# All stores from the memory stage to the end of cross-attention, issued by GpSimd instead of SyncE

## The chip, the cores and the metric

The kernel is one layer of an encoder block, written for one core of a Trainium2 chip. The core has a matrix engine (PE), a vector engine (DVE), a scalar engine (ACT), GpSimd (POOL) and SyncE (SP), which run on their own and meet at semaphores, and 16 DMA engines that move data between HBM and the on-chip memory. The metric is device time in microseconds of one launch, on one core. Each engine works through a list of instructions that is fixed when the program is built, strictly in its order: an instruction that has to wait holds up all that stand behind it on the same engine.

## The reference

The sequence has 2048 positions of width 1024, the memory 256 positions, and there is one layer. All of it is float32.

```
h  = rms_norm(x, mix_norm);  z = h @ w_in
cb, cc, cu, q, k, v, g, lr_f, lr_b = split_cols(z)
y_conv = grouped_rms_norm(cb * dwconv3(cc * cu))
o      = bidirectional_gla(q/8, k, v, log_sigmoid(lr_f @ w_af + b_af)/16, log_sigmoid(lr_b @ w_ab + b_ab)/16)
x += concat[y_conv, rms_norm(o) * silu(g)] @ w_out
kv = rms_norm(mem, mem_norm) @ w_xkv
x += softmax(rms_norm(x, xa_norm) @ w_xq . k_mem / 16) . v_mem @ w_xo        # 4 heads
x += square(relu(rms_norm(x, mlp_norm) @ w_up)) @ w_down
out = rms_norm(x, final_norm)
```

## The kernel before

Every float32 product is made of three products of a faster 32-bit format: each operand is split into a high and a low part (`split`, L115 to L118: ACT makes the high part, DVE the low one), and `mm3` (L143 to L147) issues high·high, high·low and low·high. So a weight goes from HBM into a raw tile (`load_w`, L129 to L134, the DMA is L131), through ACT and DVE, and then to PE.

The stages follow one another on PE:

- the memory stage, keys: `kv_mm` and `xa_key` for four heads make a matrix zA in HBM (8 tiles of 128x256 a head, each scaled by ACT in L565 and stored in L566). Beside it the first half of x is loaded (`load_T`, L176), squared (L184) and normalised (`block_rows`, `block_steps`).
- the first half of the projections: `qk` stores zk and zq (L234), `vg` and `lr_g` store zg and zv (`vg_store`, L253), `conv` stores zy (L371).
- the memory stage, values: `kv_mm` and `xa_value` make zO (L579 copies, L581 stores), beside it the second half of x.
- the second half of the projections, then gated linear attention for four heads (`gla_states`, `gla_out`): it reads zk, zq, zv and zg back (L420, L440, L499), runs a scan over chunks on DVE (L474), and stores zy (L515). The second half of `conv` is laid between its steps.
- the output projection with the residual, which stores x1d (L920, L908), cross-attention, which stores x2d (L731, L746), then the feed-forward layer and the last norm.

What sets the order: inside `tc.manual_schedule` the engines that it names follow the order in which the code is written; elsewhere, and for the engines it does not name, a scheduler that runs when the program is built puts the instructions of each engine in order, by costs of its own. SP issues every DMA of the kernel before the change, loads and stores, in one list. POOL has little to do in the first 2000 us: the step of the inverse root mean square in `rstd_of` (L151, L153), which takes 4 columns at a time.

Buffers come in rings by tag. A tile is given out again when all that read it are done, a store included when it has landed. The raw ring (`RAW`) has 3 buffers, `T2`, from which most stored tiles come, has 7, `GT` has 8.

Of the kernel before, what the change touches and what calls it, by code (L numbers as in the profile page):

```python
# [17 lines left out]
P = 128  # L18
# [3 lines left out]
TB = 512  # L22
EPS = 1e-6
NMEM = 256
# [6 lines left out]
def block_kernel(ctx, tc, x, mem, wm, wv, wlg, wlog, wout, wxk, wxv, wxqT, wxo, wup, wdn,  # L31
                 vecs, ones, consts, out):
    nc = tc.nc
# [70 lines left out]
    zy = [dram.tile([P, S], F32, name=f"zy{i}") for i in range(8)]  # L104
    zA = dram.tile([D, 1024], F32, name="zA")
    zO = dram.tile([1024, D], F32, name="zO")
# [120 lines left out]
    def qk(hf, blks, ws):  # L227
        t0 = hf * 1024
        for pr in range(2):
            for z, idx, sc in ((zk, 2 + pr, 1.0), (zq, pr, 0.125)):  # L230
                def ev(bi, ps, z=z, sc=sc):
                    t = T2()
                    nc.scalar.mul(t, ps, sc)
                    nc.sync.dma_start(z[pr][:, t0 + bi * TB:t0 + (bi + 1) * TB], t)  # L234
                mtiles([(idx, ev)], blks, ws)
                ws = None

# [8 lines left out]
    def vg_store(hf, t, ps, z, c, func):  # L246
        st = T2()[:, :256]
        if func is AF.Copy:
            nc.vector.tensor_copy(st, ps)  # L249
        else:  # L250
            nc.scalar.activation(st, ps, func)
        tok = hf * 1024 + t * P
        nc.sync.dma_start(z[tok:tok + P, c * 256:(c + 1) * 256], st)  # L253

    VG = ((zg, 1), (zv, 0), (zv, 1))

# [49 lines left out]
    def conv(hf, blks, cs, ws=None, meanwhile=None):  # L306

        n0 = 1022 if hf == 0 else 1026
        off = 1 if hf == 0 else 3
        a0 = 0 if hf == 0 else 1022  # L310

        def group(c, ws):
            HP, T = CV(), CV()
            if hf == 0:
                nc.vector.memset(HP[:, 0:1], 0.0)
            else:
                nc.vector.tensor_copy(HP[:, 0:3], save[:, c, 0:3])
                nc.vector.memset(HP[:, 1027:1028], 0.0)

            def ev_c(bi, ps):  # L320
                nc.scalar.copy(HP[:, off + bi * TB:off + (bi + 1) * TB], ps)

            def ev_u(bi, ps):
                sl = HP[:, off + bi * TB:off + (bi + 1) * TB]
                nc.vector.tensor_tensor(out=sl, in0=ps, in1=sl, op=ALU.mult)
                if bi == 1:
                    taps()

            def taps():

                nc.vector.tensor_scalar_mul(T[:, :n0], HP[:, 0:n0], cw[:, 3 * c:3 * c + 1])
                for tap in (1, 2):
                    nc.vector.scalar_tensor_tensor(out=T[:, :n0], in0=HP[:, tap:tap + n0],
                                                   scalar=cw[:, 3 * c + tap:3 * c + tap + 1],
                                                   in1=T[:, :n0], op0=ALU.mult, op1=ALU.add)
                if hf == 0:
                    nc.vector.tensor_copy(save[:, c, 0:3], HP[:, 1022:1025])
                else:
                    nc.vector.tensor_tensor(out=T[:, 0:2], in0=T[:, 0:2], in1=save[:, c, 4:6], op=ALU.mult)

            held = []

            def ev_b(bi, ps):
                if hf == 0 and c == 3 and bi == 0:
                    held.append(ps)
                    return
                for bj, pb in enumerate(held + [ps], start=bi - len(held)):
                    if hf == 0:
                        n = TB if bj == 0 else TB - 2
                        sl = T[:, bj * TB:bj * TB + n]  # L350
                        if bj == 1:
                            nc.vector.tensor_copy(save[:, c, 4:6], pb[:, TB - 2:TB])
                    else:
                        n = TB
                        sl = T[:, 2 + bj * TB:2 + (bj + 1) * TB]
                    nc.vector.tensor_tensor(out=sl, in0=pb[:, :n], in1=sl, op=ALU.mult)

            tiles = [(4 + 3 * c, ev_c), (5 + 3 * c, ev_u), (6 + 3 * c, ev_b)]
            if hf == 0 and c == 3:
                mtiles(tiles, blks)  # L360
            else:
                for t in tiles:
                    mtiles([t], blks, ws)
                    ws = None
                    if meanwhile and c == cs[-1]:
                        next(meanwhile, None)
            return T

        for c in cs:
            T = group(c, ws if c == cs[0] else None)  # L370
            nc.sync.dma_start(zy[c][:, a0:a0 + n0], T[:, :n0])  # L371


    def gla_decay(h, res):
# [103 lines left out]
    def gla_out(h, Q, K, St):  # L478
        ats, ys = [None] * 4, [None] * 4

        def attn(j):
            pf, pb = PG((P, 4, P)), PG((P, 4, P))
            for c in range(4):
                hf, sl = chunk(4 * j + c)
                nc.tensor.matmul(pf[:, c], K[hf][0:64, sl], Q[hf][0:64, sl], start=True, stop=True)
                nc.tensor.matmul(pb[:, c], K[hf][64:128, sl], Q[hf][64:128, sl], start=True, stop=True)
            at = ats[j] = GT(F32, (P, 4, P))
            nc.scalar.copy(at, pb)
            nc.vector.copy_predicated(at, maskf, pf)

        def outp(j):
            v = load_v(h, j)
            po = PG((P, 4, P))
            for c in range(4):
                hf, sl = chunk(4 * j + c)
                nc.tensor.matmul(po[:, c], Q[hf][:, sl], St[:, 4 * j + c], start=True, stop=False)
                nc.tensor.matmul(po[:, c], ats[j][:, c], v[:, c], start=False, stop=True)
            sg = GT(F32, (P, 4, P))
            nc.sync.dma_start(sg, zg[j * TB:(j + 1) * TB, h * P:(h + 1) * P].rearrange("(c p) d -> p c d", p=P))  # L499
            y = ys[j] = GT(F32, (P, 4, P))  # L500
            nc.scalar.activation(y, po, AF.Square)
            ss = GS(4)
            nc.vector.tensor_reduce(out=ss, in_=y, op=ALU.add, axis=AX.X)
            r = rstd_of(ss, 4, P, GS)
            for c in range(4):
                nc.vector.scalar_tensor_tensor(out=y[:, c], in0=po[:, c], scalar=r[:, c:c + 1], in1=sg[:, c],
                                               op0=ALU.mult, op1=ALU.mult)

        def fin(j):
            pt = PG((P, 4, P))  # L510
            for c in range(4):
                nc.tensor.transpose(pt[:, c], ys[j][:, c], ident)
            yt = GT(F32, (P, 4, P))
            nc.scalar.mul(yt, pt, g_gla)
            nc.sync.dma_start(zy[4 + h][:, j * TB:(j + 1) * TB], yt.rearrange("p c t -> p (c t)"))  # L515
        return attn, outp, fin


# [37 lines left out]
    def xa_key(h, K, T):  # L556
        kh, kl = K
        w = [load_w(wxqT[2 * h + j], T=T) for j in range(2)]
        for dt in range(KT):
            sl = slice(dt * P, (dt + 1) * P)  # L560
            ps = PS()
            for j in range(2):
                mm3(ps[:, :NMEM], (w[j][0][:, sl], w[j][1][:, sl]), (kh[:, j], kl[:, j]), j == 0, j == 1)
            st = T2()
            nc.scalar.activation(st[:, :NMEM], ps[:, :NMEM], AF.Copy, scale=g_xa[:, dt:dt + 1])  # L565
            nc.sync.dma_start(zA[sl, h * NMEM:(h + 1) * NMEM], st[:, :NMEM])  # L566

    def xa_value(h, V, T):
        vh, vl = V
        w = [load_w(wxo[2 * h + j], T=T) for j in range(2)]  # L570
        for m in range(2):
            for n in range(2):
# [5 lines left out]
                st = T2()  # L578
                nc.scalar.copy(st, ps)  # L579
                row = h * NMEM + m * P  # L580
                nc.sync.dma_start(zO[row:row + P, ns], st)  # L581

    def y_tiles(b, kp):
        if b == 2 and kp < 2:
# [58 lines left out]
    SB = 256  # L643
# [77 lines left out]
    def xa_out(s, q):  # L721
        L = live[s]
        xt = L["xs"][q]
        for i in range(4):
# [3 lines left out]
                ph, pl = L["p"][kt // 2]  # L728
                mm3(ps, (wO[kt][0][:, ds], wO[kt][1][:, ds]), (ph[:, kt % 2], pl[:, kt % 2]), kt == 0, kt == KT - 1)
            nc.vector.tensor_tensor(out=xt[:, i], in0=ps, in1=xt[:, i], op=ALU.add)  # L730
        nc.sync.dma_start(x2d[q * TB:(q + 1) * TB, s * SB:(s + 1) * SB].rearrange("(k p) t -> p k t", p=P), xt)  # L731

    def xa_last(s):
        L = live[s]
# [7 lines left out]
        for q in range(2):  # L742
            xt = L["xs"][q]
            for i in range(4):
                nc.vector.tensor_tensor(out=xt[:, i], in0=pss[4 * q + i], in1=xt[:, i], op=ALU.add)
            nc.sync.dma_start(x2d[q * TB:(q + 1) * TB, s * SB:(s + 1) * SB].rearrange("(k p) t -> p k t", p=P), xt)  # L746

    XR = lambda i: RAW((P, 2, TB)) if i % 2 == 0 else CV()[:, :D].rearrange("p (j t) -> p j t", j=2)

# [141 lines left out]
    for b in range(4):  # L891
        bs = slice(b * TB, (b + 1) * TB)
        yb, nxt = nxt, []
        if b == 3:
# [10 lines left out]
                    mm3(pss[d], (wo[kt][0][:, ds], wo[kt][1][:, ds]), yb[kt // 2][kt % 2], kt == 0, kt == KT - 1)  # L905
            for d in range(KT):
                nc.vector.tensor_tensor(out=xts[d], in0=pss[d], in1=xts[d], op=ALU.add)
                nc.sync.dma_start(x1d[d * P:(d + 1) * P, bs], xts[d])  # L908
            continue
        for dp in range(KT // 2):  # L910
            ld = y_load(b + 1, dp)
            xt = load_T(x, b, dp, CV()[:, :D].rearrange("p (j t) -> p j t", j=2))
            for j in range(2):
# [3 lines left out]
                for kt in range(KT):  # L917
                    mm3(ps, (wo[kt][0][:, ds], wo[kt][1][:, ds]), yb[kt // 2][kt % 2], kt == 0, kt == KT - 1)
                nc.vector.tensor_tensor(out=xt[:, j], in0=ps, in1=xt[:, j], op=ALU.add)
                nc.sync.dma_start(x1d[ds, bs], xt[:, j])  # L920
            nxt.append(y_split(b + 1, dp, *ld))

    row = lambda z, kt: z[kt * P:(kt + 1) * P, :]
# [488 lines left out]
```

## Time and profile before

| what | value |
|---|---|
| time, median of 3 runs (lowest to highest) | 2677.62 us (2676.23 to 2678.01) |
| time of the profiled execution | 2673.82 us |
| its span | 2672.0 us |
| PE busy | 2580.3 us, 97% of the span |
| DVE, ACT, POOL busy | 61%, 35%, 10% |
| granted clock of PE, mean over the span | 0.988 |
| DMA queue of SP | 351.05 MB, 40.2% of 16 engines' span |
| POOL instructions | 178 in all |

The profile comes from one execution of the program; the span is the time between its first and last instruction, and some 2 us lie around it. "Busy" counts instructions of the engine itself, and not what its sequencer does: waits and the issue of DMAs show in rows marked with a q (SPq). In the timeline a row gives the start in us from the beginning of the span, the duration, engine and line, operation, the tiles written and read, and in square brackets the idle time just before it with what ended it; "x5" means that five instructions were merged into the row, with the duration from the first start to the last end.

### The profile page before, as it was taken

The numbers are of one execution on the slowest core, as the hardware profiler recorded it, in microseconds if no ns is written. First come the engines' busy times: TensorE is split into PE (matmuls) and PEld (weight loads), VectorE is DVE, ScalarE is ACT, GpSimd is POOL, SyncE is SP. The second block draws the span as 40 slices with busy tenths as digits, with TensorE's granted clock in tenths as the row PEclk, the third lists the DMA queues.
The fourth block names the chain that finished last, engine by engine and source line by source line (L and its number), as shares of the span: only waits on it lengthen the run. The fifth ranks groups of instructions, "written<-read, shape, count | busy, mean of one in ns | idle before, by whom it ended". The sixth has DMA issues, their size and how long they took to land.

```text
span 2672.0 us, 34688 instructions
## 1 busy us (share of the span) xinstructions
PE 2580.3 (97%) x13560; PEld 2199.2 (82%) x13560; DVE 1627.1 (61%) x2502; ACT 934.0 (35%) x1432; POOL 259.9 (10%) x178
## 2 busy tenths in 40 slices
PE   7999999989989999999999999999999999999998
PEld 7898888877777787999997888788887888888887
DVE  6512364367766555444468566865555768788887
ACT  6411143334435443232225333443333323222322
POOL 0000000000000000000000000000002324243233
PEclk9999999999999999999999999999999999999999
DMA  7512355234445453110125333343328664555232
GB/s 258 179 60 67 107 175 174 74 91 127 123 117 171 146 181 111 46 50 33 64 79 185 115 107 114 111 161 111 122 99 309 229 196 156 179 162 183 95 116 106
DMA packets 198308, 353.26 MB, mean 132 GB/s; under 512 B 17344, under 2 KB 73792, under 8 KB 198144
## 3 DMA queue, kind: packets, MB, share of 16 engines
q1 hardware_dynamic: 198144, 351.05, 40.2%
q8 instruction: 106, 1.74, 0.3%
q14 instruction: 58, 0.48, 0.1%
HBM read 262.90 MB, written 88.08 MB: 131 GB/s over the span
## 4 chain that ended last, share of the span: by engine, by line
PE 79%; DVE 10%; DMA 5%; ACT 3%; issue 2%; POOL 1%; SPq 0%; DVEq 0%; POOLq 0%; ACTq 0%
PE ps L1016 12%; PE pg L1260 10%; PE ps L1260 10%; PE ps L145 9%; PE ps L147 9%; PE ps L146 9%; PE pg L1016 9%; PE pg L145 2%; PE pg L146 2%; PE pg L147 2%; DVE a L118 2%; DMA gt<-zv 1%; DVE st L474 1%; DMA raw<-zy 1%; DVE a L928 1%
## 5 line engine op out<-in xcount | busy, mean ns | idle before, releaser
L145 PE MATMUL ps<-a,a 128*128 128x512 f32 (+1 forms) x840 | 306.1, 364 | 6.4 <-DVE t L249 5.9
L146 PE MATMUL ps<-a,a 128*128 128x512 f32 (+1 forms) x840 | 306.0, 364 | 0.0
L147 PE MATMUL ps<-a,a 128*128 128x512 f32 (+1 forms) x840 | 305.0, 363 | 0.0
L1260 PE MATMUL pg<-a,g 128*128 128x512 f32 x1176 | 285.8, 389 | 3.6 <-DVE a L928 1.2
L1016 PE MATMUL ps<-a,g 128*128 128x512 f32 x1152 | 282.6, 390 | 2.5 <-DVE a L118 1.4
L1260 PE MATMUL ps<-a,g 128*128 128x512 f32 x1176 | 284.9, 389 | 0.0
L1016 PE MATMUL pg<-a,g 128*128 128x512 f32 x1152 | 278.4, 389 | 1.7 <-ACT g L117 1.1
L1260 PEld LDWEIGHTS pg<-a,g 128*128 128x128 f32 x1176 | 220.4, 188 | 51.3 <-ACT a L117 2.8
L1260 PEld LDWEIGHTS ps<-a,g 128*128 128x128 f32 x1176 | 220.7, 188 | 45.8
L1016 PEld LDWEIGHTS ps<-a,g 128*128 128x128 f32 x1152 | 215.9, 188 | 48.5 <-DVE a L118 2.1
L1016 PEld LDWEIGHTS pg<-a,g 128*128 128x128 f32 x1152 | 215.9, 188 | 48.1 <-ACT g L117 2.0
L117 ACT CAST a<-raw 128x1024 fp32r<-128x1024 f32 (+1 forms) x128 | 130.0, 1022 | 331.2 <-PE ps L1260 102.6
L118 DVE TENSOR_TENSOR a<-raw,a 128x1024 fp32r<-128x1024 f32 (+1 forms) x128 | 156.3, 1228 | 122.9 <-ACT a L117 121.1
L117 ACT CAST g<-gt 128x512 fp32r<-128x512 f32 x180 | 103.8, 618 | 334.8 <-PE pg L1016 192.8
L145 PEld LDWEIGHTS ps<-a,a 128*128 128x128 f32 x840 | 161.5, 192 | 32.6 <-DVE t L249 4.7
L147 PEld LDWEIGHTS ps<-a,a 128*128 128x128 f32 x840 | 161.8, 193 | 23.2
L146 PEld LDWEIGHTS ps<-a,a 128*128 128x128 f32 x840 | 161.8, 193 | 23.2 <-issue 0.2
L118 DVE TENSOR_TENSOR g<-gt,g 128x512 fp32r<-128x512 f32 x180 | 129.7, 758 | 49.1 <-ACT g L117 49.0
L928 DVE TENSOR_TENSOR t<-pg,t 128x512 f32<-128x512 f32 x64 | 44.2, 690 | 166.6 <-issue 127.9
L153 POOL TENSOR_TENSOR sm<-sm,nhalf 128x2 f32<-128x2 f32 (+1 forms) x26 | 24.3, 933 | 991.2 <-DVE sm L151 991.2
L118 DVE TENSOR_TENSOR g<-raw,g 128x1024 fp32r<-128x1024 f32 (+3 forms) x90 | 98.6, 1106 | 34.8 <-ACT g L117 34.6
L117 ACT CAST g<-raw 128x1024 fp32r<-128x1024 f32 (+3 forms) x90 | 85.4, 959 | 97.6 <-PE ps L146 17.7
(325 smaller groups left out, 5203.0 us busy)
## 6 DMA issues: line engine op xcount, KB each, us to landing
raw<-zu SPq DMA_DIRECT2D x64, 512.0 KB, 4.0
t<-in_wdn SPq DMA_DIRECT2D x84, 256.0 KB, 3.7
raw<-in_wm SPq DMA_DIRECT2D x32, 512.0 KB, 4.0
raw<-in_wup SPq DMA_DIRECT2D x32, 512.0 KB, 4.1
cv<-in_wup SPq DMA_DIRECT2D x32, 512.0 KB, 5.0
zu<-gt SPq DMA_DIRECT2D x64, 256.0 KB, 2.3
zu<-t SPq DMA_DIRECT2D x64, 256.0 KB, 3.9
cv<-zu SPq DMA_DIRECT2D x32, 512.0 KB, 5.1
```

The source lines that it names most:

```text
L117: mark["act"] = nc.scalar.copy(hi, src)
L118: nc.vector.tensor_tensor(out=lo, in0=src, in1=hi.bitcast(F32), op=ALU.subtract)
L145: nc.tensor.matmul(ps, lh, rh, start=first, stop=False)
L146: nc.tensor.matmul(ps, lh, rl, start=False, stop=False)
L147: mark["pe"] = nc.tensor.matmul(ps, ll, rh, start=False, stop=last)
L153: nc.gpsimd.tensor_tensor(out=r, in0=v, in1=nhalf[:, :n], op=ALU.pow)
L474: nc.vector.scalar_tensor_tensor(out=St[r, a], in0=St[r, b], scalar=de[r, a:a + 1], in1=St[r, a], op0=ALU.mult, op1=ALU.add)
L928: eng.tensor_tensor(out=out, in0=a, in1=b, op=op)
L1016: nc.tensor.matmul(ps, W[w][:, ks], X[x][kt], start=first and kt + w + x == 0, stop=kt == 3 and w == 1, skip_group_check=not first)
L1260: nc.tensor.matmul(ps, l, r, start=not chained and k == 0 and l is wh and r is x[k][0], stop=k == n - 1 and l is wl, skip_group_check=chained)
```

## The change

Ten `dma_start` calls move from `nc.sync` to `nc.gpsimd`: those that store zk and zq, zg and zv, zy (two places), zA, zO, x1d (two places) and x2d (two places). These are 200 DMAs at run time. The stores of the feed-forward layer (zu) and of the output stay on SP. Nothing else is edited.

```diff
-                    nc.sync.dma_start(z[pr][:, t0 + bi * TB:t0 + (bi + 1) * TB], t)
+                    nc.gpsimd.dma_start(z[pr][:, t0 + bi * TB:t0 + (bi + 1) * TB], t)
...
-        nc.sync.dma_start(z[tok:tok + P, c * 256:(c + 1) * 256], st)
+        nc.gpsimd.dma_start(z[tok:tok + P, c * 256:(c + 1) * 256], st)
...
-            nc.sync.dma_start(zy[c][:, a0:a0 + n0], T[:, :n0])
+            nc.gpsimd.dma_start(zy[c][:, a0:a0 + n0], T[:, :n0])
...
-            nc.sync.dma_start(zy[4 + h][:, j * TB:(j + 1) * TB], yt.rearrange("p c t -> p (c t)"))
+            nc.gpsimd.dma_start(zy[4 + h][:, j * TB:(j + 1) * TB], yt.rearrange("p c t -> p (c t)"))
...
-            nc.sync.dma_start(zA[sl, h * NMEM:(h + 1) * NMEM], st[:, :NMEM])
+            nc.gpsimd.dma_start(zA[sl, h * NMEM:(h + 1) * NMEM], st[:, :NMEM])
...
-                nc.sync.dma_start(zO[row:row + P, ns], st)
+                nc.gpsimd.dma_start(zO[row:row + P, ns], st)
...
-        nc.sync.dma_start(x2d[q * TB:(q + 1) * TB, s * SB:(s + 1) * SB].rearrange("(k p) t -> p k t", p=P), xt)
+        nc.gpsimd.dma_start(x2d[q * TB:(q + 1) * TB, s * SB:(s + 1) * SB].rearrange("(k p) t -> p k t", p=P), xt)
...
-                nc.sync.dma_start(x1d[d * P:(d + 1) * P, bs], xts[d])
+                nc.gpsimd.dma_start(x1d[d * P:(d + 1) * P, bs], xts[d])
...
-                nc.sync.dma_start(x1d[ds, bs], xt[:, j])
+                nc.gpsimd.dma_start(x1d[ds, bs], xt[:, j])
```

How the lists of the engines change shows in three places. The first is SP's list in the memory stage for values, where the second quarter of x is loaded (a_3223 to a_3232, from in_x), the four tiles of one head are stored into zO, and the weights of the next head come in (in_wxv, in_wxo). Lines with a minus stand in the list before, lines with a plus in the list after.

```order
 L176 DMA a_3232<-in_x 128x512 x2
-L581 DMA zO<-t_3190 128x512
-L131 DMA raw<-in_wxv 128x1024
-L581 DMA zO<-t_3200 128x512
-L581 DMA zO<-t_3210 128x512
-L131 DMA raw<-in_wxv 128x1024
-L581 DMA zO<-t_3220 128x512
-L131 DMA raw<-in_wxo 128x1024 x3
+L131 DMA raw<-in_wxv 128x1024 x2
+L131 DMA raw<-in_wxo 128x1024 x4
```

The loads keep their order among themselves, and no store stands between them any more. In the memory stage for keys SP's list changes in the same way (zA, in_wxk, in_wxqT, in_x).

The second place is POOL's list in the memory stage for keys, around the inverse root mean square (L153) that belongs to the second quarter of x. The stores ahead of it are those of the third head, the ones behind it those of the fourth; before, the four rows of L153 with 4 columns stood there with nothing between them.

```order
+L566 DMA zA<-t_740 128x256
+L566 DMA zA<-t_750 128x256
+L566 DMA zA<-t_760 128x256
+L153 TENSOR_TENSOR sm<-sm,nhalf 128x4
+L566 DMA zA<-t_828 128x256
+L566 DMA zA<-t_838 128x256
```

Now L153 comes after the last of eight stores of one head. In the stage for values it stands behind the twelfth store of zO in the same way.

The third place is DVE's list in the attention, at the scan of the last head (L474; L489 copies a masked product, L603 to L635 belong to the norm of the first block of zy). Before:

```order
L474 SCALAR_TENSOR_TENSOR st<-st,gs 64x128 x8
L489 COPY_PREDICATED gt<-cst,pg 128x512
L474 SCALAR_TENSOR_TENSOR st<-st,gs 64x128
L603 TENSOR_TENSOR t_6857<-t_6857,ps 128x512
L474 SCALAR_TENSOR_TENSOR st<-st,gs 64x128
L489 COPY_PREDICATED gt<-cst,pg 128x512
L474 SCALAR_TENSOR_TENSOR st<-st,gs 64x128
L604 TENSOR_SCALAR t_6857<-t_6857 128x512
L474 SCALAR_TENSOR_TENSOR st<-st,gs 64x128
L605 TENSOR_TENSOR t_6833<-t_6857,t_6833 128x512
```

And after, at the same place:

```order
L474 SCALAR_TENSOR_TENSOR st<-st,gs 64x128 x8
L489 COPY_PREDICATED gt<-cst,pg 128x512
L474 SCALAR_TENSOR_TENSOR st<-st,gs 64x128 x3
L489 COPY_PREDICATED gt<-cst,pg 128x512
L474 SCALAR_TENSOR_TENSOR st<-st,gs 64x128 x6
L503 TENSOR_REDUCE gs<-gt 128x4
```

The norm's instructions no longer stand between the steps of the scan; they come after it. PE's list changes too, in the attention alone: pieces of the convolution's matmuls stand a little earlier or later between the attention's. From cross-attention on, the lists of PE and DVE are as they were.

More of the change, by code (lines that the diff above doesn't have):

```diff
@@ L745, in xa_last @@
                 nc.vector.tensor_tensor(out=xt[:, i], in0=pss[4 * q + i], in1=xt[:, i], op=ALU.add)
-            nc.sync.dma_start(x2d[q * TB:(q + 1) * TB, s * SB:(s + 1) * SB].rearrange("(k p) t -> p k t", p=P), xt)
+            nc.gpsimd.dma_start(x2d[q * TB:(q + 1) * TB, s * SB:(s + 1) * SB].rearrange("(k p) t -> p k t", p=P), xt)
     XR = lambda i: RAW((P, 2, TB)) if i % 2 == 0 else CV()[:, :D].rearrange("p (j t) -> p j t", j=2)
```

## The prediction

> **What bounds the kernel now.** I read the busy time of each engine by stage first. The columns are the stage in us, its length, then busy us and instructions of PE, PE's weight loads, DVE, ACT and POOL, then the granted clock of PE, the share of the DMA engines and GB/s.
>
> ```profile
> 0.00:75.00 75.00, 55.33 (x387) 52.76 (x388) 50.75 (x68) 47.39 (x70) 2.91 (x7) 0.93 0.75 244
> 75.00:350.00 275.00, 274.97 (x1585) 244.56 (x1585) 78.57 (x112) 54.09 (x76) 0.00 (x0) 0.99 0.30 97
> 350.00:400.00 50.00, 45.23 (x291) 41.79 (x290) 35.63 (x41) 31.69 (x41) 2.02 (x2) 0.93 0.69 231
> 500.00:850.00 350.00, 313.51 (x1914) 265.15 (x1914) 240.87 (x480) 142.44 (x190) 21.53 (x32) 0.97 0.41 123
> ...
> 1050.00:1350.00 300.00, 299.91 (x1977) 271.68 (x1976) 136.27 (x309) 89.86 (x204) 10.67 (x12) 1.00 0.14 46
> 1350.00:2672.00 1322.00, 1298.22 (x6026) 1080.03 (x6024) 943.05 (x1276) 447.51 (x672) 221.38 (x123) 1.00 0.45 148
> ```
>
> PE is the bound wherever it has data: in the 275 us after 75 and in cross-attention (1050 to 1350) it is idle for 0.1 us at most, so 60 of the 200 moved stores (44 of the first half's projections and the 16 of x2d) lie where nothing can be gained. The idle time that the change can reach is in the two memory stages (0 to 75, where the first 11 us are the first loads; 350 to 400) and in the attention (36.5 us in 500 to 850). The last row, half of the kernel, is not touched.
>
> An idle gap costs more than itself. I asked for the clock right behind four of the gaps named below:
>
> ```profile
> 44.60:47.90 3.30, 3.27 (x15) 3.27 (x16) 0.00 (x0) 1.80 (x4) 0.00 (x0) 0.51 0.40 137
> 61.70:65.00 3.30, 3.30 (x18) 3.30 (x17) 3.30 (x5) 1.66 (x5) 0.00 (x0) 0.50 0.87 278
> 382.50:389.20 6.70, 6.05 (x26) 5.76 (x27) 5.83 (x7) 4.17 (x6) 0.00 (x0) 0.51 0.73 251
> 795.60:798.90 3.30, 3.11 (x14) 3.14 (x15) 3.20 (x6) 0.93 (x2) 0.00 (x0) 0.50 0.00 0
> ```
>
> PE runs at half its clock there, for 3.3 or 6.7 us, so such a gap loses another 1.65 or 3.35 us.
>
> **Term 1, weights of the key stage: -4.2 us.** The rows are splits of weights on DVE, then SP's list, then rows of PE that open with an idle gap.
>
> ```profile
> 30.47 2.35 DVE L118 TENSOR_TENSOR a<-raw,a 128x1024 fp32r<-128x1024 f32 x2
> 33.26 1.23 DVE L118 TENSOR_TENSOR a<-raw,a 128x1024 fp32r<-128x1024 f32 x1 [0.44 <-ACT a L117]
> ...
> 36.94 1.23 DVE L118 TENSOR_TENSOR a<-raw,a 128x1024 fp32r<-128x1024 f32 x1 [1.86 <-ACT a L117]
> ```
>
> ```profile
> 31.72 0.33 SPq L131 DMA_DIRECT2D raw<-in_wxk  x1
> 32.14 2.87 SPq L566 DMA_DIRECT2D zA<-t  x5
> 35.10 0.89 SPq L131 DMA_DIRECT2D raw<-in_wxqT  x2
> ...
> 48.41 1.18 SPq L566 DMA_DIRECT2D zA<-t  x2
> 49.68 0.45 SPq L131 DMA_DIRECT2D raw<-in_wxqT  x1
> ```
>
> ```profile
> 42.08 0.39 PE L145 MATMUL ps<-t,g 128*128 128x256 f32 x1 [1.91 <-ACT g L117]
> 43.34 0.39 PE L147 MATMUL ps<-t,g 128*128 128x256 f32 x1 [0.76 <-DVE g L118]
> 44.63 0.58 PE L147 MATMUL ps<-t,g 128*128 128x256 f32 x1 [0.67 <-DVE g L118]
> ...
> 59.52 0.39 PE L145 MATMUL ps<-t,g 128*128 128x256 f32 x1 [0.72 <-ACT g L117]
> 60.78 0.39 PE L147 MATMUL ps<-t,g 128*128 128x256 f32 x1 [0.76 <-DVE g L118]
> ```
>
> A weight load needs a raw buffer, which the DVE half of an earlier split frees. For the two loads at 35.10 and 35.58 the buffers came free at 32.8 and 34.5, while SP stood at five stores of zA. Without these the second, on which PE's gap before 44.6 ends, goes 1.1 us earlier. The load at 49.68 stood behind a store that waited for ACT; its buffer had been free for some 11 us (the split that ends at 38.17). So both gaps at 58.7 to 60.8 (0.72 + 0.76 = 1.48) go, with the half clock behind them (1.65). Bounds: nothing, and 8.1 if all of the gaps from 40 on went (1.91 + 0.76 + 0.67 = 3.34, and 1.48, and two windows of 1.65).
>
> **Term 2, weights of the value stage: -6.3 us.**
>
> ```profile
> 367.92 4.26 SPq L176 DMA_DIRECT2D a<-in_x  x8
> 375.93 0.33 SPq L581 DMA_DIRECT2D zO<-t  x1
> 376.35 0.38 SPq L131 DMA_DIRECT2D raw<-in_wxv  x1
> ...
> 375.34 0.56 ACT L579 COPY t<-ps 128x512 f32<-128x512 f32 x1
> ```
>
> ```profile
> 382.69 0.58 PE L145 MATMUL ps<-gt,g 128*128 128x256 f32 x1 [2.96 <-ACT g L117]
> ```
>
> SP was free at 372.2 and then waited 3.8 us to store a tile that ACT copied only at 375.34. The load behind it carries the weights for which PE then idles 2.96 us. Issued at 372.2 it lands 4.1 us earlier, which covers the gap and, with it, the 6.7 us of half clock. Bounds: nothing (if the raw buffer is late), and 6.3.
>
> **Term 3, loads of the attention: -2.8 us.**
>
> ```profile
> 548.48 14.12 SPq L253 DMA_DIRECT2D zv<-t  x6
> 566.33 15.31 SPq L440 DMA_DIRECT2D gt<-zv  x5
> 571.94 1.13 PE L465 MATMUL pg<-gt 128*128 128x128 f32 x8 [1.55 <-DMA gt<-zv]
> 758.82 1.14 SPq L515 DMA_DIRECT2D zy<-gt  x1
> 765.79 0.49 PE L497 MATMUL pg<-gt 128*128 128x128 f32 x2 [2.56 <-DMA gt<-zv]
> ```
>
> The first load of zv stood behind stores of zv that follow PE's pace for 14 us; it can go well before 566, and the gap of 1.55 goes. Of the gap of 2.56 the store at 758.82 accounts for 1.2 (1.14 and the issue around it). The other gaps there end on DVE, on POOL's root mean square, or on loads that waited for their own buffer, so they stay. Bounds: nothing, and 4.1 (both gaps).
>
> **Term 4, the scan of the last head: -6.0 us.**
>
> ```profile
> 782.61 3.02 DVE L474 SCALAR_TENSOR_TENSOR st<-st,gs 64x128 f32<-64x128 f32 x8
> 795.29 0.35 DVE L474 SCALAR_TENSOR_TENSOR st<-st,gs 64x128 f32<-64x128 f32 x1
> 795.79 0.76 PE L496 MATMUL pg<-st,g 128*128 128x128 f32 x2 [4.38 <-DVE st L474]
> ```
>
> The scan took from 782.61 to 795.64, as the list before has a step of the norm after each step of the scan. In the list after, 17 steps at 3.02/8 = 0.38 us and two L489 of 0.76 end 8.0 us after the start, at 790.6, ahead of PE's gap (791.4). So the 4.38 us go, and the half clock behind them (1.65). Bounds: nothing (if what is now behind the scan is late instead), and 6.0.
>
> **Cost 1, POOL's stores: +4.2 us.** No row shows a DMA that POOL issues. The first row below is from the list of PE's waits, the last from the DMA issues (KB each, us from issue to landing). Call x the time by which such a store is later done than SP's.
>
> ```profile
> PE pg L169 <- POOL sm L153: 5.7, 4, 1.8
> ```
>
> ```profile
> 69.17 1.01 POOL L153 TENSOR_TENSOR sm<-sm,nhalf 128x4 f32<-128x4 f32 x1 [27.71 <-DVE sm L151]
> ...
> 61.99 6.94 SPq L566 DMA_DIRECT2D zA<-t  x8
> ...
> zA<-t SPq DMA_DIRECT2D x32, 128.0 KB, 3.0
> ```
>
> First, the stored tiles of zA come from a ring of seven, two of which hold the head's keys; five are left. Each is held for ACT's 0.5, the issue (6.94/8 = 0.87) and the landing of 3.0: 4.4 us, and five in 4.4 us is a tile every 0.87 us, the very pace of the row. So x delays each of 32 tiles by x/5, 6.4x in all. Second, L153 stands right behind stores in both memory stages, and PE's wait list (total us, times, longest) has it waiting for L153 four times, of which I count one in each stage: 2x. The price is 8.4x. Bounds: x = -0.5, a store that never waits behind a load and takes as little as SP's shortest issue (0.33), and x = 3.0, a landing twice as long. I take 0.5: POOL's small operation takes 1.01 us where SP's issue takes 0.33 to 0.87. In the attention POOL gets 20 stores (16 of L515, 4 of the convolution) among 16 root mean squares, and is busy for 21.53 of 350 us: 20 issues of 1.0 us each fit into what is left, so I count nothing there.
>
> In the Trainium skill, "DMA: Bandwidth & Descriptors", section "Specifications", the first byte comes after about 1 us for a DMA of GpSimd and 0.6 us for one of SyncE. By that page x would be about 0.4 (an estimate), and cost 1 3.4 us instead of 4.2.
>
> **Cost 2, the new order: +2 us.** The matmuls of the convolution and many splits change places. PE's total work is the same; where a gap opens or closes I can price only term 4. I take one more gap of the usual size (1.3 to 2.0 us), with bounds of -2 and +12.
>
> **Sum.** -4.2 - 6.3 - 2.8 - 6.0 + 4.2 + 2.0 = -13.1 us. Against the profiled execution (2673.82) that is 2660.7; it lies 3.8 us under the median of the runs, and against this (2677.62) I forecast **2664.5**.
>
> **Rivals.**
>
> *A: the loads are bound by their buffers.* With three raw buffers SP would wait for DVE where it now waits behind a store. For it: the load at 31.72 went out as DVE freed a buffer (half of 2.35 after 30.47 is 31.65), and the attention's loads often do. Against it: the loads of terms 1 and 2 went out 0.04 us after a store. Terms 1 to 3 are then nothing and the sum is -6.0 + 4.2 + 2.0 = +0.2: 2677.8. In the Trainium skill, the same page, section "Issuing engines are not separate DMA queues", says that issuing from several engines saves only the sequencer's time to issue. By that rule the time would be as in this rival; the rows show otherwise in that an issue which waits for its data holds the loads behind it for 3.8 us.
>
> *B, the slower side: POOL's stores are slow.* The place is the ring of stored tiles in the key stage and L153 behind it, the price 8.4 us for each us of x. From x = 2.7 on (13.1 + 4.2 + 5.4, over 8.4) the kernel is slower by over 0.2%; at x = 3.0 it is 2664.5 + 2.5 x 8.4 = 2685.5. For it: no row excludes it. Against it: the same DMA engines move the same bytes, whichever engine issues them. In the Trainium skill, "SBUF — State Buffer", section "Who interferes with whom", GpSimd cannot write a DMA's descriptors while DVE runs certain operations on two ports, which would lengthen x; no row here shows it.
>
> *C: the new order opens gaps.* Two gaps like the 4.38 with their half clock add 12 us to the sum: 2676.6.
>
> **How the numbers follow.** A measurement of this kernel can tell about 0.2%, 5.4 us, from no change. Forecast 0.60, A 0.17, B 0.14, C 0.09. Faster: the forecast and a little of A, 0.62. Within 0.2%: most of A and C, 0.22. Slower: B with the edges of A and C, 0.16. The low end takes the far bounds of term 1 (3.9 more), x = -0.5 (8.4) and cost 2 at -2 (4.0), less what these can hardly give together: 2650. The high end takes in A and C and the nearer part of B: 2685. Left out is some 0.17.
>
> **What would show it.** Right: no gap of PE ended by ACT's split at 380 and at 59; the clock full at 382 to 389; the wait for L474 at 791 gone; SP's loads of weights waiting on DVE alone. Wrong: PE idle at those places still, with the load late for its buffer (A); ACT's L565 waiting for a buffer, PE's tiles of zA further apart than 0.87 us, L169 waiting longer for L153 than its 1.8 us of before (B); PE gaps at new places in 500 to 850 (C). I would be wrong altogether if stores by POOL held up cross-attention, where PE has had no idle time.

## The result, and the profile after

| | before | after |
|---|---|---|
| median of 5 runs (lowest to highest), us | 2676.23 (2669.78 to 2678.01) | 2689.31 (2686.01 to 2689.62) |
| ratio, 95% interval | 1 | 1.0049 (1.0036 to 1.0061) |
| profiled execution: span, us | 2672.0 | 2684.2 |

The kernel became slower by 0.49%, 13 us, and the time lies 4.3 us above the range. These are the busy times by stage after the change, in the columns used before.

```profile
0.00:75.00 75.00, 53.86 (x391) 51.29 (x392) 51.53 (x69) 47.21 (x71) 17.08 (x31) 0.93 0.71 248
...
350.00:400.00 50.00, 43.52 (x284) 38.44 (x284) 36.97 (x42) 34.12 (x43) 8.62 (x14) 0.98 0.75 242
...
500.00:850.00 350.00, 309.66 (x1887) 261.80 (x1886) 238.96 (x476) 140.84 (x189) 42.65 (x71) 0.97 0.39 121
```

PE was busy for less of each of these stages than before (53.86 against 55.33 us, 43.52 against 45.23, 309.66 against 313.51), though the idle time there was to shrink. Busy time alone does not say what was lost: from 0 to 75 us PE got through 391 matmuls instead of 387. So the next table sets the profiled executions against that of the kernel before at the same matmul of PE: numbers 800, 2800, 4800, 5200, 5600, 7600 and 8400 of 13560 start at 149, 496, 866, 965, 1059, 1359 and 1508 us before. A cell is what PE lost (+) or won (-) between two of them, in us.

| run | to 149, keys | to 496, values | to 866, attention | to 965 | to 1059, start of cross-attention | to 1359 | to 1508, start of feed-forward |
|---|---|---|---|---|---|---|---|
| after | -1.8 | -0.3 | +4.7 | -0.7 | +4.8 | 0.0 | +4.4 |
| e1 old order | +0.4 | +1.0 | +2.8 | -3.5 | +1.0 | +0.8 | +2.7 |
| e2 new order, SP | -1.5 | +0.3 | +3.1 | -5.0 | +6.2 | +0.8 | +1.7 |
| e3 larger room | +1.2 | -0.8 | +3.2 | -0.3 | +5.7 | 0.0 | +3.0 |
| e4 x1d, x2d on SP | -0.7 | +0.3 | +5.4 | -3.1 | -0.2 | +0.8 | +1.6 |
| e6 old order from L907 | +0.6 | -1.5 | +3.1 | -1.7 | -1.5 | +0.8 | +5.4 |
| e7 scan alone | +0.4 | -0.4 | +3.5 | +0.1 | +0.2 | +0.8 | +0.2 |
| e9 only x1d | +0.4 | -0.3 | +0.7 | -1.1 | +7.5 | 0.0 | -0.3 |
| e10 only x2d | -1.1 | -0.1 | +2.7 | -1.9 | -0.5 | 0.0 | +3.9 |
| e11 only memory stages | -0.1 | -1.3 | +1.3 | -0.6 | -0.2 | +0.8 | +1.7 |
| e12 only attention | +2.2 | +0.2 | +1.0 | -1.2 | +0.4 | 0.0 | +0.2 |

Between two executions a stage varies by itself: e10 does in the attention what the kernel before does, and differs there by 2.7; e11 does so at the start of the feed-forward layer, and differs by 1.7. In the attention every run loses against this one execution of the kernel before, so that column says as much of this execution as of the runs. Only the start of cross-attention and that of the feed-forward layer stand out. Cross-attention between them lost nothing.

**The memory stage for keys.** Rows of PE, DVE and POOL after the change; the last is PE's row before.

```profile
64.50 0.95 PE L161 MATMUL pg<-vec,a 128*128 128x1 f32 x8
70.26 2.08 PE L169 MATMUL pg<-cst,sm 128*128 128x128 f32 x8 [4.81 <-POOL sm L153]
...
66.89 1.23 DVE L118 TENSOR_TENSOR a<-a,a 128x1024 fp32r<-128x1024 f32 x1 [0.45 <-ACT a L117]
68.03 0.16 DVE L151 TENSOR_SCALAR sm<-pg 128x4 f32<-128x4 f32 x1
68.10 1.22 DVE L118 TENSOR_TENSOR a<-a,a 128x1024 fp32r<-128x1024 f32 x1
...
68.27 1.94 POOL L153 TENSOR_TENSOR sm<-sm,nhalf 128x4 f32<-128x4 f32 x1 [1.18 <-DVE sm L151]
```

```profile
70.23 1.16 PE L169 MATMUL pg<-cst,sm 128*128 128x128 f32 x8 [1.76 <-POOL sm L153]
```

PE came to L169 three us earlier than before (65.45 against 68.47: 70.26 - 4.81 and 70.23 - 1.76) and left the wait at the same time. The sums that L161 makes were there at 65.45, but L151, which reads them, stood on DVE behind the splits of x until 68.03. L153 took 1.94 us instead of 1.01 besides. No store held it: the last one ahead of it was out at 67.10. What PE had won by then, the norm of x took back.

Rival B's sign showed too, but small: ACT's L565 waited three times, 4.2 us in all, for a zA store to land, which it never did before, and PE waited 1.0 us for L565 (0.3 before). One of the places:

```profile
50.63 0.47 ACT L565 ACTIVATE t<-ps,vec 128x256 f32<-128x256 f32 x1 [1.72 <-DMA zA<-t]
51.16 0.39 PE L145 MATMUL ps<-gt,a 128*128 128x256 f32 x1 [0.32 <-ACT t L565]
```

**Values.** SP's load of the weights, and PE's gaps behind it.

```profile
368.57 0.98 SPq L131 DMA_DIRECT2D raw<-in_wxv  x2
...
378.05 0.50 PE L145 MATMUL ps<-g,t 128*128 128x512 f32 x1 [2.40 <-ACT t L579]
...
397.25 1.36 PE L169 MATMUL pg<-cst,sm 128*128 128x128 f32 x8 [3.23 <-POOL sm L153]
```

The load goes out 7.8 us earlier (368.57 against 376.35), and the gap of 2.96 us is gone. But it lands only 3.9 us earlier (377.66 against 381.57): it now goes out right behind eight loads of x, and takes 9.1 us from issue to landing where it took 5.2. First after, then before:

```profile
DMA to landing us min/median/max: 9.1/9.1/9.1
...
DMA to landing us min/median/max: 5.2/5.2/5.2
```

Nor did the load alone close the gap. In the experiment e1, which keeps the old lists of PE, DVE and ACT, it goes out at 370.88 and lands 9.0 us later, at 379.89, and PE waits at the old place:

```profile
381.79 0.39 PE L145 MATMUL ps<-gt,g 128*128 128x256 f32 x1 [1.63 <-ACT g L117]
...
384.50 0.38 PE L147 MATMUL ps<-gt,g 128*128 128x256 f32 x1 [2.22 <-DVE g L118]
```

In the changed kernel other waits stand in its place: PE waits 2.40 us for ACT's copies, which the new order puts behind the squares of x, and 3.23 us (1.34 before) for L153.

**The first load of zv**, in SP's list and in SP's waits between 555 and 570 us (total us, times, longest):

```profile
561.92 2.06 SPq L131 DMA_DIRECT2D raw<-in_wm  x2
564.15 2.94 SPq L440 DMA_DIRECT2D gt<-zv  x4
```

```profile
SPq L131 <- DVE a L118: 22.9, 1, 22.9
```

No store stands ahead of it now, but two weight loads do, the first of which waits 22.9 us for a raw buffer. It went out at 564.15 instead of 566.33, while PE was 2.1 us ahead: nothing won.

**The last scan**, DVE and PE:

```profile
775.85 3.02 DVE L474 SCALAR_TENSOR_TENSOR st<-st,gs 64x128 f32<-64x128 f32 x8
...
781.61 2.29 DVE L474 SCALAR_TENSOR_TENSOR st<-st,gs 64x128 f32<-64x128 f32 x6
...
784.04 0.77 PE L496 MATMUL pg<-st,g 128*128 128x128 f32 x2 [2.36 <-DVE st L474]
```

The scan takes 8.05 us (775.85 to 783.90), where 8.0 were forecast and 13.0 measured before. But PE's list has less to do meanwhile: it runs dry 5.8 us after the scan's start, before it was 8.8, so 2.36 us of the gap stay.

**The start of cross-attention.** DVE, with the row of ACT that it waits for, and PE:

```profile
1027.43 1.04 ACT L117 CAST a<-raw 128x1024 fp32r<-128x1024 f32 x1 [4.74 <-DMA raw<-zO]
...
1028.50 1.22 DVE L118 TENSOR_TENSOR a<-raw,a 128x1024 fp32r<-128x1024 f32 x1 [0.37 <-ACT a L117]
1029.65 0.68 DVE L907 TENSOR_TENSOR gt<-pg,gt 128x512 f32<-128x512 f32 x1
...
1042.28 0.61 PE L161 MATMUL pg<-vec,t 128*128 128x1 f32 x4 [3.05 <-DVE t L655]
```

A split of zO's weights now stands ahead of the last L907, so the last tile of x1d, the norm and the splits of x1 behind it are late. PE's second L161 stands three matmuls earlier and waits for them. The section on the change said that the lists of PE and DVE are as before from cross-attention on; that was wrong, they differ at this place and at the stores of x2d.

**The start of the feed-forward layer**: POOL, SP, and the time from issue to landing (lowest, median, highest) of the first and of the second store.

```profile
1411.39 0.75 POOL L746 DMA_DIRECT2D x2d<-raw  x1 [26.66 <-DVE cv L745]
1415.05 0.76 POOL L746 DMA_DIRECT2D x2d<-cv  x1 [2.90 <-DVE g L118]
1415.83 0.72 POOL L153 TENSOR_TENSOR sm<-sm,nhalf 128x2 f32<-128x2 f32 x1
...
1421.81 0.80 SPq L993 DMA_DIRECT2D cv<-in_wup  x2
```

```profile
DMA to landing us min/median/max: 3.4/3.4/3.4
...
DMA to landing us min/median/max: 6.7/6.7/6.7
```

The first store lands at 1414.8 (1411.39 + 3.4), and only then the second is issued, though DVE had written its data by 1412.3. (The row names DVE's L118; by the experiment e3 it is the landing.) L153 behind it is as late, and the second store, now behind weight loads, needs 6.7 us where SP's needed 3.1, so the loads of in_wup that reuse its buffer go out at 1421.81; they went at 1407.85 before, with PE 6.8 us ahead of where it is now. Behind them on SP stands the load of x2d for the next block (1423.52, before 1413.74), for which DVE waits, and PE for DVE. The first two rows are from after, the last two from before:

```profile
1429.81 0.75 DVE L960 SCALAR_TENSOR_TENSOR st<-st,vec,rows 128x512 f32<-128x512 f32 x1 [3.30 <-DMA st<-x2d]
1431.82 4.14 PE L1016 MATMUL pg<-a,g 128*128 128x512 f32 x10 [2.38 <-DVE g L118]
```

```profile
1417.83 0.75 DVE L960 SCALAR_TENSOR_TENSOR st<-st,vec,rows 128x512 f32<-128x512 f32 x1 [1.10 <-DMA st<-x2d]
1419.84 2.57 PE L1016 MATMUL pg<-a,g 128*128 128x512 f32 x10 [0.16 <-DVE g L118]
```

A gap of 1.08 us at 1417.93, behind the late L153, comes on top; before there was none.

### The profile page after: what moved, and what is told of

It reads as the page before. It is cut to its first block, busy times and chain, and to the rows that moved or that the text cites. A ratio compares the mean times of both kernels' runs of the same rounds, so it can differ in the third digit from the quotient of the medians.

```text
span 2684.2 us, 34836 instructions
## 1 busy us (share of the span) xinstructions
PE 2583.1 (96%) x13560; PEld 2198.3 (82%) x13560; DVE 1626.5 (61%) x2502; ACT 933.7 (35%) x1432; POOL 376.1 (14%) x378
## 4 chain that ended last, share of the span: by engine, by line
PE 77%; DVE 8%; issue 5%; DMA 5%; ACT 3%; POOL 1%; SPq 0%; POOLq 0%; DVEq 0%; ACTq 0%
PE ps L1016 12%; PE ps L1260 10%; PE pg L1260 10%; PE pg L1016 9%; PE ps L145 9%; PE ps L146 9%; PE ps L147 9%; PE pg L145 2%; PE pg L147 2%; PE pg L146 2%; DMA gt<-zv 1%; DVE a L118 1%; DVE st L474 1%; DVE a L928 1%; ACT a L117 1%
## 5 line engine op out<-in xcount | busy, mean ns | idle before, releaser
L118 DVE TENSOR_TENSOR a<-raw,a 128x1024 fp32r<-128x1024 f32 (+1 forms) x128 | 158.2, 1243 | 123.3 <-ACT a L117 121.0
L118 DVE TENSOR_TENSOR g<-gt,g 128x512 fp32r<-128x512 f32 x180 | 127.4, 746 | 48.6 <-ACT g L117 48.4
L118 DVE TENSOR_TENSOR g<-raw,g 128x1024 fp32r<-128x1024 f32 (+3 forms) x90 | 98.6, 1108 | 34.2 <-ACT g L117 33.9
L117 ACT CAST g<-raw 128x1024 fp32r<-128x1024 f32 (+3 forms) x90 | 85.3, 961 | 95.1 <-PE ps L146 17.6
L928 POOL TENSOR_TENSOR st<-st,raw 128x1024 f32<-128x1024 f32 x8 | 21.6, 2696 | 673.0 <-DMA raw<-zu 673.0
```

Of the source, the lines that this page charges most:

```text
L117: mark["act"] = nc.scalar.copy(hi, src)
L118: nc.vector.tensor_tensor(out=lo, in0=src, in1=hi.bitcast(F32), op=ALU.subtract)
L928: eng.tensor_tensor(out=out, in0=a, in1=b, op=op)
```

## The experiments

The kernel before was measured anew beside each group of runs (its medians are 2673.59 to 2676.36 us), so runs are compared by their ratio to it. The first two hold an engine's list to an order that is written out, by edges that set the order of issue alone:

```diff
         block_kernel(tc, *args, res)
+        keep_order(tc)
...
+                tc.add_manual_dep(traced[f"I-{n}"], before, mybir.DependencyInfo(
+                    mybir.DependencyClass.NoSync, mybir.DependencyReason.DATA), reason="order")
+            before = f"I-{n}"
```

**e1**, the changed kernel in the old order.

> The changed kernel, with PE, DVE and ACT held to the instruction order of the kernel before; all ten kinds of store still go out by POOL. Theory O (what costs is the new order of PE, DVE and ACT that came with the change: 4.7 us in the attention, 4.8 us where cross-attention begins): the memory stages keep their gain of 2.1 us and nothing is lost, 2674 us; with the 4.4 us that the feed-forward layer's start lost to POOL's store of x2d still there, 2678 us. Theory Q (what costs is that POOL's list and its queue hold stores, root mean squares and buffers back): the losses stay where they are, 2687 to 2690 us.

Measured: 2684.46, ratio 1.0034 (1.0022 to 1.0045). Neither theory held: with the old order, too, POOL's stores cost about two thirds.

**e2**, the kernel before in the new order.

> The kernel before (every store by SP), with PE, DVE and ACT held to the instruction order of the changed kernel. Theory O: it is slow without a single store on POOL, 2676 + 4.7 + 4.8 = 2685 us, with PE idle before L161 at 1040 again. Theory Q: as the kernel before, 2674 to 2678 us.

Measured: 2685.93, ratio 1.0035 (1.0022 to 1.0048), as theory O says, with no store on POOL:

```profile
1024.01 1.23 DVE L118 TENSOR_TENSOR a<-raw,a 128x1024 fp32r<-128x1024 f32 x1 [0.99 <-ACT a L117]
...
1036.96 0.92 PE L161 MATMUL pg<-vec,t 128*128 128x1 f32 x4 [4.46 <-DVE t L655]
```

So both parts cost, each about 0.35% alone and together 0.49%. In e1, whose lists of PE and DVE are the old ones there, PE has no gap at the second L161: the start of cross-attention is lost to the order. SP's list is held in neither run; in e2 it follows the new order in part, and the loads of in_wxv go out at 371.34 with every store still on SP. Not all of either loss is placed: e1's 0.34% is some 9 us, and its profile, 4.3 us under its median, shows 2.7 at the start of the feed-forward layer and the rest within what stages vary by.

**e3**, more room for descriptors.

```diff
-    nc = bacc.Bacc("TRN2", target_bir_lowering=False, num_devices=1, dynamic_dma_scratch_size=1024)
+    nc = bacc.Bacc("TRN2", target_bir_lowering=False, num_devices=1, dynamic_dma_scratch_size=1408)
```

> The changed kernel with the memory that POOL's queue has for the descriptors of its transfers raised from 1024 to 1408 bytes a partition, and nothing else. In the changed kernel the second store of x2d in L746 goes out 0.3 us after the first has landed, and the root mean square behind it on POOL and the weight load behind its buffer are late. If the room for descriptors holds it (one such store at a time), the second store goes out within 1 us of its data, and the start of the feed-forward layer gets up to 4.4 us back: 2685 us. If it is something else that holds it: 2689 us, the second store still behind the landing of the first.

```profile
1414.17 0.75 POOL L746 DMA_DIRECT2D x2d<-raw  x1 [27.20 <-DVE cv L745]
1415.50 0.75 POOL L746 DMA_DIRECT2D x2d<-cv  x1 [0.57 <-DVE sm L151]
```

The second store goes out 1.33 us after the first, before that has landed: the room held it. It lands after 4.0 us instead of 6.7. PE's gap of 1.08 us is gone and the one of 2.38 is 0.65:

```profile
1431.52 2.60 PE L1016 MATMUL pg<-a,g 128*128 128x512 f32 x10 [0.65 <-DVE g L118]
```

So the held store opened these two gaps. The time, 2686.39 and ratio 1.0042 (1.0028 to 1.0055), is lower by 2.9 us, which the intervals do not tell apart from nothing.

**e4**, of the changed kernel, x1d and x2d back on SP; **e9** and **e10**, of the kernel before, only x1d or only x2d on POOL; **e11** and **e12**, only the memory stages or only the projections and the attention. One line of each edit is shown.

```diff
-        nc.gpsimd.dma_start(x2d[q * TB:(q + 1) * TB, s * SB:(s + 1) * SB].rearrange("(k p) t -> p k t", p=P), xt)
+        nc.sync.dma_start(x2d[q * TB:(q + 1) * TB, s * SB:(s + 1) * SB].rearrange("(k p) t -> p k t", p=P), xt)
```

> The changed kernel with the stores of x1d and x2d back on SP (L908, L920, L731, L746). If the losses at the start of cross-attention (4.8 us) and of the feed-forward layer (4.4 us) belong to these stores: 2689.3 - 9.2 = 2680 us, PE without the gap of 3.05 us before L161. If they only show what was late already: 2687 to 2690 us.

```diff
-                nc.sync.dma_start(x1d[d * P:(d + 1) * P, bs], xts[d])
+                nc.gpsimd.dma_start(x1d[d * P:(d + 1) * P, bs], xts[d])
```

> The kernel before, with the stores of x1d alone (L908, L920) by POOL; the order of PE and DVE at the start of cross-attention is then that of the changed kernel, the rest as before. If the loss there is these stores' doing and independent of the rest: the gap before L161 near 1035 us, and 4.8 us more, 2674 + 4.8 = 2679 us. If it needs the delays from earlier stages: within 1 us of the kernel before.

```diff
-            nc.sync.dma_start(x2d[q * TB:(q + 1) * TB, s * SB:(s + 1) * SB].rearrange("(k p) t -> p k t", p=P), xt)
+            nc.gpsimd.dma_start(x2d[q * TB:(q + 1) * TB, s * SB:(s + 1) * SB].rearrange("(k p) t -> p k t", p=P), xt)
```

> The kernel before, with the stores of x2d alone (L731, L746) by POOL. If the start of the feed-forward layer is lost to them alone (the second store of L746 behind the landing of the first, the root mean square and the loads of in_wup behind it): the gaps of PE near 1410 to 1430 us, and 4.4 us more, 2678 us. If not: 2673 to 2676 us.

```diff
-                nc.sync.dma_start(zO[row:row + P, ns], st)
+                nc.gpsimd.dma_start(zO[row:row + P, ns], st)
```

> The kernel before, with the stores of the memory stages alone (zA, zO) by POOL, PE's list as before. By the stages of the changed kernel's trace: 2.1 us less, 2672 us, no difference that can be told from none. My terms 1 and 2 as predicted would have been 10.5 us less at a cost of 4.2: 2668 us.

```diff
-        nc.sync.dma_start(z[tok:tok + P, c * 256:(c + 1) * 256], st)
+        nc.gpsimd.dma_start(z[tok:tok + P, c * 256:(c + 1) * 256], st)
```

> The kernel before, with the stores of the projections and of the attention alone (zk, zq, zg, zv, zy) by POOL; PE's and DVE's lists in the attention are then nearly those of the changed kernel. By the stages of the changed kernel's trace: 4.0 us more from 525 to 965 us, 2678 us. My terms 3 and 4 would have been 8.8 us less: 2665 us.

| stores by POOL | median, us | ratio (95%) |
|---|---|---|
| all but x1d, x2d (e4) | 2679.79 | 1.0012 (1.0001 to 1.0022) |
| x1d (e9) | 2680.50 | 1.0015 (1.0006 to 1.0025) |
| x2d (e10) | 2680.64 | 1.0013 (1.0004 to 1.0022) |
| memory stages (e11) | 2676.23 | 0.9999 (0.9990 to 1.0008) |
| projections and attention (e12) | 2677.49 | 1.0006 (0.9997 to 1.0016) |

With x1d and x2d on SP, 0.37 of the 0.49% are gone; each costs by itself, and where the trace had it:

```profile
1041.11 1.00 PE L161 MATMUL pg<-vec,t 128*128 128x1 f32 x4 [3.71 <-DVE t L655]
```

```profile
1402.81 0.76 POOL L746 DMA_DIRECT2D x2d<-raw  x1 [25.77 <-DVE cv L745]
1406.47 0.76 POOL L746 DMA_DIRECT2D x2d<-cv  x1 [2.90 <-DVE g L118]
```

The first row is e9's, the others are e10's. To move a store also moves the order that comes with it, so these runs alone do not part the two. The other 152 stores, on which all four of my terms rest, win nothing, neither the memory stages' nor the rest.

**e5**, the norm of x earlier. DVE's list in the changed kernel, edited (and L153 on POOL ahead of the last stores):

```diff
 L206 SCALAR_TENSOR_TENSOR a_390<-a_390,vec,t_609 128x512
+L151 TENSOR_SCALAR sm<-pg 128x4
 L206 SCALAR_TENSOR_TENSOR a_390<-a_390,vec,t_609 128x512
 L118 TENSOR_TENSOR a_776<-a_387,a_775 128x1024
-L151 TENSOR_SCALAR sm<-pg 128x4
```

> The changed kernel, with one step moved in each memory stage: L151 of the stage's second quarter of x stands two (for keys) and one (for values) DVE instructions and one split earlier, and L153 on POOL ahead of the last two stores of zA and the last of zO; the rest of every list as in the changed kernel. Theory N (the loads did come earlier, and PE gave the time back waiting for the norm of x, whose L151 stood behind DVE's other work): the gaps of 4.81 and 3.23 us before L169 shrink to about 2.5 and 1.7 us, 2689.3 - 2.3 - 1.5 = 2685.5 us. Rival (something else is as late, so the time turns up in the next gap): 2688 to 2690 us.

```profile
68.82 1.16 PE L169 MATMUL pg<-cst,sm 128*128 128x128 f32 x8 [2.06 <-POOL sm L153]
72.22 0.58 PE L145 MATMUL ps<-t,g 128*128 128x256 f32 x1 [2.24 <-ACT t L117]
74.39 0.58 PE L146 MATMUL ps<-t,g 128*128 128x256 f32 x1 [1.59 <-DVE t L118]
...
400.09 1.16 PE L169 MATMUL pg<-cst,sm 128*128 128x128 f32 x8 [3.20 <-POOL sm L153]
```

Measured: 2689.98, ratio 1.0056 (1.0044 to 1.0069), no gain. For keys the wait fell to 2.06 us as said, and 3.83 us (2.24 + 1.59) opened right behind it for the next split. For values it stayed: there L153 took 2.60 us.

**e6**, the old order from L907 on.

```diff
 L907 TENSOR_TENSOR gt<-ps,gt 128x512
-L118 TENSOR_TENSOR a_8515<-raw,a_8514 128x1024
 L907 TENSOR_TENSOR gt<-pg,gt 128x512
```

> The changed kernel, with the instruction order of PE, DVE and ACT from the output projection's end on (L907 and later) as in the kernel before; up to there the new order, and all stores by POOL. Theory O for the start of cross-attention (the split of zO's weights that now stands ahead of the last L907 holds DVE until its load has landed): the gap of 3.05 us before L161 goes, with the half clock behind it: 2689.3 - 4.8 = 2684.5 us. Rival (the landing of POOL's x1d stores, from which the buffers for the splits come): the gap stays at 2 us or more, 2687 to 2690 us.

Measured: 2681.26, ratio 1.0027 (1.0018 to 1.0036). The wait before L161 fell to 1.60 us though all of x1d is stored by POOL. It is the order.

```profile
1036.69 0.61 PE L161 MATMUL pg<-vec,t 128*128 128x1 f32 x4 [1.60 <-DVE t L655]
```

By the ratios 0.22% came back, 5.9 us. The profile has all of it at the start of cross-attention (-1.5 instead of +4.8). The edit takes back the new order at the stores of x2d as well, but at the start of the feed-forward layer nothing came back (+5.4 instead of +4.4).

**e7**, the scan alone, in DVE's list of the kernel before.

```diff
 L474 SCALAR_TENSOR_TENSOR st<-st,gs 64x128
-L603 TENSOR_TENSOR t_6857<-t_6857,ps 128x512
 L474 SCALAR_TENSOR_TENSOR st<-st,gs 64x128
...
 L474 SCALAR_TENSOR_TENSOR st<-st,gs 64x128
+L603 TENSOR_TENSOR t_6857<-t_6857,ps 128x512
```

> The kernel before (every store by SP), with one edit in DVE's list: the 17 steps of the last head's scan and its two L489 follow one another, and the eight steps of the norm that stood between them come behind; PE's list stays as before. My term 4 by itself: the gap of 4.38 us goes and its half clock with it, 2676.4 - 6.0 = 2670.4 us. Rival (the norm, 5 us later, is then what PE waits for, at L512 or L626): 2675 to 2678 us.

```profile
802.22 0.45 PE L512 MATMUL pg<-cst,gt 128*128 128x128 f32 x1 [5.79 <-DVE gt L506]
```

Measured: 2675.59, ratio 1.0002 (0.9992 to 1.0012). The gap of 4.38 us is gone and one of 5.79 us stands 10 us further on, for L506, which stands behind the norm's steps. DVE has the same work either way.

**e8**, the kernel before with e7's edit, e5's earlier L151, and DVE and ACT in the memory stages in the new order; of DVE's list:

```diff
-L151 TENSOR_SCALAR sm<-pg 128x4
 L118 TENSOR_TENSOR g_496<-raw,g_495 128x1024
 L118 TENSOR_TENSOR g_502<-raw,g_501 128x1024
+L151 TENSOR_SCALAR sm<-pg 128x4
```

> The kernel before (every store by SP), with three pieces of order: DVE and ACT in the two memory stages as in the changed kernel, L151 earlier there as in the run with the early norm, and the last scan uninterrupted. If these three are what the changed kernel had to win, and none needs POOL's stores: 2676.4 - 1.5 - 3 - 5 = 2667 us. If they need the loads that only stores off SP set free: 2672 to 2676 us.

Measured: 2679.33, ratio 1.0019 (1.0010 to 1.0028): slower. No run was faster than the kernel before.

## Why the prediction was wrong

The forecast was 13.1 us faster, and the kernel became 13 us slower. Two steps failed. Each term took an idle gap of PE as won, with nothing behind it that would be late in its turn; and the two costs looked for their price elsewhere: cost 1 in the memory stages, cost 2 as one gap of the usual size, from 500 to 850 us. The losses that stand out lie at the two ends of cross-attention, in no term.

- **Terms 1 and 2** (-10.5). The loads did go out earlier, and their gaps went or shrank. Two things were wrong. An earlier issue is neither an equally earlier landing nor an equally earlier split: in the value stage 7.8 us of issue became 3.9 of landing, and in e1 5.5 became 1.7; in the key stage of e1 the weights for which PE waits 1.72 us at 60.98 landed 8.5 us earlier (49.95 against 58.40), and DVE split them no earlier (59.70 against 59.50), where its old list has them. And nothing else was to be late: I let the waits for L153, 1.76 and 1.34 us, stand as they were, when PE would reach them sooner and L151 would not. e11 shows the two terms and their cost together as nothing.
- **Term 3** (-2.8). The row read "behind stores for 14 us"; behind these stood two loads that wait for a buffer. It was rival A's mechanism, which I had given to another place.
- **Term 4** (-6.0). The scan was right to 0.1 us. That PE would still have its 8.8 us of work ahead of the gap was not: I took PE's list from before, knowing that it had changed. e7 shows that even with the old list the time turns up behind the scan, as the bound of the term said that gave it nothing.
- **Cost 1** (+4.2). For zA x was too high: the issue takes 0.55 us (17.6 us for 32 stores of zA), and the landing 2.7 us instead of 3.0. The ring in the key stage, the place of rival B, held ACT for 4.2 us and PE for some 0.7; the price came at x2d, where a store holds L153 and the weight loads.
- **Cost 2** (+2). Rival C's kind of cost, but I looked for it from 500 to 850 us alone. The largest piece is at 1030, outside of every term.
- That cross-attention cannot gain was right. That it therefore does not matter was the error: its stage rows show no idle time, but its two ends have waits that a reordered list can lengthen.

Shown are the two places and their mechanisms. For x1d it is the order of DVE and PE (e2, e6, e9). For x2d it is the held store: e10 has it alone, e1 and e6 have it with the old order and lose there too, and e3 closes the gaps. How much time it costs is less sure, since e3's gain is within the intervals; whether the order adds to it cannot be told (without the held store e2, in the new order, loses 1.7 there, e4 and e11, in the old one, 1.6 and 1.7). The four parts alone sum to 0.33%, all together make 0.49%; whether the rest is their joint effect is open, since the intervals are about 0.1% each. Open, too, is where e1 and e2 lose what their profiles do not place.

## What to carry to other kernels

When a stall is to go, name the next wait in the same stage and the instruction that feeds it: it does not move by itself, and it takes the gain. Where a scheduler places instructions, a change of the issuing engine is also a change of order; compare the whole lists, the joints between stages above all. An engine that is idle still serves one list: a store that waits there holds the small operation behind it.

## What was not expected of the hardware

POOL's L153 on four columns took 1.01 to 1.04 us, and 1.92 to 2.60 in several runs, e2 among them, which has no store on POOL. The long ones begin beside an L118, L188 or L206 on DVE, the short ones beside an L552 or an idle DVE:

```profile
68.89 1.92 POOL L153 TENSOR_TENSOR sm<-sm,nhalf 128x4 f32<-128x4 f32 x1 [24.72 <-DVE sm L151]
...
68.72 1.22 DVE L118 TENSOR_TENSOR a<-a,a 128x1024 fp32r<-128x1024 f32 x1
```

```profile
397.44 2.60 POOL L153 TENSOR_TENSOR sm<-sm,nhalf 128x4 f32<-128x4 f32 x1 [0.90 <-DVE sm L151]
```

The first fence is e2's, the second e5's. In the Trainium skill, "SBUF — State Buffer", section "Who interferes with whom", a DVE instruction with two inputs in SBUF contends with a GpSimd instruction that reads SBUF. These rows agree: L118 reads two such tiles, L552 one from PSUM. Each lengthened L153 ended about 0.9 us after such a DVE instruction: 1.94 us beside an L118 with 1.05 left (the changed kernel), 1.45 beside an L206 with 0.58 left (e8). An L118 that began 0.44 us after L153 did not lengthen it (1.01, the kernel before). It was not tested by itself.

POOL's issue of a store of x2d (512 KB) took 0.75 to 0.80 us, of the other stores 0.54 to 0.60. It does not go by the bytes alone: the stores of zy with 511 and 513 KB took 0.56. With 1024 bytes a partition for its descriptors, one of the last two stores of x2d was under way at a time (1414.8 against 1415.05); with 1408, both.
